# Modulation sums turned by transposes, an earlier first weight split, and narrower chunks in a decoder step on one core

## The chip, the cores and the metric

The kernel runs on one core of one Trainium2 chip. TensorE (PE in the profile) multiplies, VectorE (DVE), ScalarE (ACT) and GpSimd (POOL) do the element-wise work, SyncE (SP) issues most DMAs. The metric is the device time of one execution in microseconds. Three runs of the kernel before took 1521.88, 1522.25 and 1519.98 us; the median is 1521.88.

## The reference

One layer of a decoder runs for 256 prompt tokens and 8 sample tokens that share all weights. The parts that matter here are the modulation and the large products:

```
mod = silu(c) @ w_ada + b_ada                    # 2048 x 12288
sh1, sc1, gt1, sh2, sc2, gt2 = split(mod, 6)     # parts 0 to 5
h = rmsnorm(x, g) * (1 + sc1) + sh1
q, k, v, u, ga, gb = split(h @ w_in)             # 2048 x 9216
...                                              # attention, pooling, gates: mix
x = x + gt1 * (mix @ w_out)                      # 2048 x 2048
h2 = rmsnorm(x, g2) * (1 + sc2) + sh2
x = x + gt2 * (square(relu(h2 @ w_mlp_up)) @ w_mlp_down)   # 2048 x 8192 and back
```

After that comes a final RMSNorm. All is float32, and the caches of keys, values and pooling rows are outputs too.

## The kernel before, in words

Activations lie transposed: 16 blocks of 128 model rows (kt) by N = 264 columns, 256 of the prompt and 8 of the samples. Every weight tile is loaded by `load` (L218) into one of 5 buffers named raw, 1 MB at most. `split_w` (L226) splits 1024 columns of it into hi (a cast on ACT, L230) and lo (a subtraction on DVE, L231), in one of 3 buffers each. `mm3` (L238) then makes one product as three: hi by hi, hi by lo, lo by hi (L241 to L243). Results lie in 5 PSUM buffers (`mm_tile`).

The modulation is a product with 9 columns (one prompt, 8 samples). TensorE holds 32 columns of cT and streams w_ada past it, in four column groups at once, so the result pa has 9 used rows in each of four 32-row groups. `ada_block` (L251) copies pa to SBUF on ACT. A function `finish` turns it into columns: each block of 128 columns is multiplied by a 0/1 selection matrix, sel2 or sel4 (L311, L356). `set_mods` (L256) adds b_ada on DVE, and for the two scale parts (1 and 4) adds 1 and multiplies by the norm weight. `ada_pair` (L271) makes parts 0 and 1 for the rows of one chunk; `ada_part` (L330) makes one whole later part in 16 steps. Two tiles of w_ada are consumed in one burst (L263). A `finish` waits in `pending` until `flush` runs, at the next load of a modulation tile or before a use.

The first 40 of the 72 column blocks of w_in are computed in chunks of kt: CHUNKS = (1, 1, 2, 4, 4, 4), at L487. A chunk of n rows of blocks goes over all 40 column blocks, n kt deep, and adds its part sums to qkv and up in SBUF. In chunk 0 ACT writes every block (L503). In chunks up to PI = 2 every third block goes through ACT and POOL (L506, L507), all others through DVE (L509, L511). While chunk i runs, `ada_pair` for chunk i + 1 is fed between its units (L527 to L533), and before the last unit `mod_in` makes the rows of h for chunk i + 1: on DVE x times R (L460), on ACT scale and shift (L464), on DVE the sample columns (L465, L466), then `split_x` into hi on ACT and lo on DVE (L235, L236). The first `mod_in(0)` stands ahead of the loop at L520, after the first `ada_pair`, six warm-up transposes (L440) and the row statistics.

The last chunk, the gates, and the projections of the pooling and attention branches are woven with the steps of the later modulation parts in the order 2, 4, 3, 5 (`late`, L519). The output projection (L902) has 16 units and takes a late step after every second one, WO = (1, 2). `need(3)` at L904 then makes sure that part 3 is there. Its columns are appended to h2 (L905, L906), and the MLP starts; its first 512 columns use rows that are not yet normalised, and correct the result later. In the MLP one late step follows every third unit, TW = (1, 3); behind the last part come copies of the caches.

The program's instructions are not issued strictly in the order written: a planner orders each engine's queue by the written order and by what it reckons to be ready, and the engines then work each queue in order. `issue_after` pins one behind another.

Of the kernel before, what the change touches and what calls it, by code (L numbers as in the profile page):

```python
# [22 lines left out]
F32 = mybir.dt.float32  # L23
# [17 lines left out]
CHUNKS = (1, 1, 2, 4, 4, 4)  # L41
# [5 lines left out]
WO = (1, 2)  # L47
TW = (1, 3)
MB = 5
PI, PM = 2, 3  # L50
# [5 lines left out]
def _consts():  # L56
# [12 lines left out]
    sel2, sel4 = np.zeros((128, 18)), np.zeros((128, 36))  # L69
    for g in range(4):  # L70
        for j in range(9):
            sel2[32 * g + j, g // 2 * 9 + j] = 1
            sel4[32 * g + j, g * 9 + j] = 1
    put("sel2", sel2)
    put("sel4", sel4)
# [49 lines left out]
def step_kernel(ctx, tc, x_prompt, x_sample, vectors, c_sample, kv0, kv1, kv2, state_pool, w_ada, w_in, w_up_attn,  # L125
# [37 lines left out]
    def con(name, rows=128):  # L163
        a, n = CONSTS[name]
        i = sum(a >= m for m in _MARKS)
        a -= ([0] + _MARKS)[i]
        return ctiles[i][:rows, a:a + n]
# [3 lines left out]
    sel2, sel4 = con("sel2"), con("sel4")  # L171
# [83 lines left out]

    def set_mods(part, d0, m, p):  # L256
        n = m.shape[1]
        nc.vector.tensor_add(m, p, bT[:, part * 16 + d0:part * 16 + d0 + n, None].to_broadcast([128, n, 9]))
        if part in (1, 4):
            gv = (g_mix if part == 1 else g_mlp)[:, d0:d0 + n, None].to_broadcast([128, n, 9])  # L260
            nc.vector.scalar_tensor_tensor(m, m, 1.0, gv, op0=OP.add, op1=OP.mult)
# [9 lines left out]
    def ada_pair(d0, n, per=2):  # L271
# [34 lines left out]
        def finish():  # L306
            sel = sel2 if n == 1 else sel4
            f = sel.shape[1]
            p = mm_tile()[:, :cols // 128 * f].rearrange("p (a b) -> p a b", b=f)
            for j in range(cols // 128):  # L310
                nc.tensor.matmul(p[:, j], sb[:, j * 128:(j + 1) * 128], sel, start=True, stop=True)  # L311
            for g in range(0, 4, 2 if n == 1 else 1):
                part, half = divmod(g, 2)
                dd = d0 + half * (cols // 128)
                c = g // 2 * 9 if n == 1 else g * 9
                m = mods[:, part * 16 + dd:part * 16 + dd + cols // 128]
                set_mods(part, dd, m, p[:, :, c:c + 9])
# [12 lines left out]
    def ada_part(part):  # L330
# [22 lines left out]
        def finish():  # L353
            p = mm_tile()[:, :144].rearrange("p (j g i) -> p g j i", j=4, g=4)
            for j in range(4):
                nc.tensor.matmul(p[:, :, j], sb[:, j * 128:(j + 1) * 128], sel4, start=True, stop=True)  # L356
            ready.add(part)
            for g in range(4):
                set_mods(part, 4 * g, mods[:, part * 16 + 4 * g:part * 16 + 4 * g + 4], p[:, g])
# [6 lines left out]
    nc.vector.tensor_copy(bT, p1)  # L366
    p1 = px([128, 128])
# [119 lines left out]
    def in_chunk(i):  # L487
        d0, n = starts[i], CHUNKS[i]
        w = 2048 // n
        for c0 in range(0, NB1 * 128, w):  # L490
            ww = min(w, NB1 * 128 - c0)
            v = load(w_in[d0 * 128:(d0 + n) * 128, c0:c0 + ww], n, ww)
            for q0 in range(0, ww, 1024 // n):
                wq = split_w(v[:, :, q0:q0 + 1024 // n])
                for j in range(8 // n):
# [6 lines left out]
                    if i == 0:  # L502
                        nc.scalar.activation(dst, ps, AF.Copy, scale=sc)  # L503
                    elif i <= PI and blk % PM == 1:
                        t = spare[:, blk // PM % 3]
                        nc.scalar.activation(t, ps, AF.Copy, scale=sc)  # L506
                        nc.gpsimd.tensor_add(dst, dst, t)  # L507
                    elif blk < 12:
                        nc.vector.scalar_tensor_tensor(dst, ps, sc, dst, op0=OP.mult, op1=OP.add)  # L509
                    else:  # L510
                        nc.vector.tensor_add(dst, dst, ps)  # L511
# [5 lines left out]

    starts = [sum(CHUNKS[:i]) for i in range(len(CHUNKS))]
    late = chain(*[ada_part(p) for p in (2, 4, 3, 5)])  # L519
    mod_in(0)  # L520
    for i, n in enumerate(CHUNKS):
        units = -(-n * NB1 // 16)
        if i + 1 < len(CHUNKS):
# [3 lines left out]
            for u, _ in enumerate(in_chunk(i)):  # L527
# [542 lines left out]
```

## Time and profile before

| | |
|---|---|
| median of three runs | 1521.88 us |
| profiled execution | 1521.63 us |
| its span, first to last instruction | 1519.9 us |
| busy: TensorE, weight loads, DVE, ACT, POOL | 1492.5, 1401.5, 860.4, 665.6, 86.4 us |
| mean granted TensorE clock | 0.994 of full |
| DMA | 377.63 MB, mean 248 GB/s |

Rows of a timeline give the start and the length in us, the engine, the line, what is written and read, a count (x), and in brackets how long the engine stood idle before and what ended that. Rows with A:B give busy time and, as (x), instructions of PE, weight load, DVE, ACT and POOL in a stretch, then the granted clock, the busy share of the DMA engines and GB/s. SPq is SP's DMA queue, with the time an issue took.

### The profile page before, as it was taken

The numbers are of one execution on the slowest core, as the hardware profiler recorded it, in microseconds if no ns is written. First come the engines' busy times: TensorE is split into PE (matmuls) and PEld (weight loads), VectorE is DVE, ScalarE is ACT, GpSimd is POOL, SyncE is SP. The second block draws the span as 40 slices with busy tenths as digits, with TensorE's granted clock in tenths as the row PEclk, the third lists the DMA queues.
The fourth block names the chain that finished last, engine by engine and source line by source line (L and its number), as shares of the span: only waits on it lengthen the run. The fifth ranks groups of instructions, "written<-read, shape, count | busy, mean of one in ns | idle before, by whom it ended". The sixth has DMA issues, their size and how long they took to land.

```text
span 1519.9 us, 29037 instructions
## 1 busy us (share of the span) xinstructions
PE 1492.5 (98%) x12349; PEld 1401.5 (92%) x12349; DVE 860.4 (57%) x1358; ACT 665.6 (44%) x985; POOL 86.4 (6%) x147
## 2 busy tenths in 40 slices
PE   7999999999999999999999999999999999999997
PEld 6889999877799988999899999999999999999997
DVE  4766656544466436765765445545555455555765
ACT  6543433344434534454554444344343443434455
POOL 0320000010011000300000000000010000100000
PEclk9999999999999999999999999999999999999998
DMA  9898788887797778767666666666567585777641
GB/s 287 305 334 295 258 315 282 300 291 269 270 317 255 263 261 305 280 248 251 206 223 229 232 235 228 230 234 229 189 230 239 201 297 175 260 239 241 237 139 58
DMA packets 161395, 377.63 MB, mean 248 GB/s; under 512 B 7234, under 2 KB 25170, under 8 KB 151657
## 3 DMA queue, kind: packets, MB, share of 16 engines
q1 hardware_dynamic: 151616, 340.02, 65.1%
q0 software_dynamic: 4064, 33.05, 6.0%
q10 hardware_dynamic: 5584, 2.69, 0.6%
q8 instruction: 97, 1.59, 0.4%
q14 instruction: 34, 0.27, 0.1%
HBM read 370.75 MB, written 26.15 MB: 261 GB/s over the span
## 4 chain that ended last, share of the span: by engine, by line
PE 95%; ACT 2%; DMA 2%; DVE 0%; issue 0%; ACTq 0%; SPq 0%
PE mm L241 29%; PE mm L242 28%; PE mm L243 28%; PE pa L339 4%; PE pa L289 2%; DMA raw<-in_w_in_dram 1%; DMA raw<-in_w_ada_dram 1%; ACT whi L230 1%; PE px L624 1%; ACT qkv L503 1%; PE px L642 0%; PE px L637 0%; PE px L982 0%; PE px L430 0%; PE px L803 0%; PE mm L356 0%
## 5 line engine op out<-in xcount | busy, mean ns | idle before, releaser
L231 DVE TENSOR_TENSOR wlo<-raw,whi 128x1024 fp32r<-128x1024 f32 x448 | 552.0, 1233 | 479.3 <-ACT whi L230 478.7
L230 ACT CAST whi<-raw 128x1024 fp32r<-128x1024 f32 x448 | 469.2, 1049 | 646.6 <-PE mm L242 554.6
L241 PE MATMUL mm<-hhi,whi 128*128 128x264 f32 x1152 | 331.8, 290 | 3.3 <-ACT whi L230 3.3
L242 PE MATMUL mm<-hlo,whi 128*128 128x264 f32 x1152 | 329.6, 287 | 0.0
L243 PE MATMUL mm<-hhi,wlo 128*128 128x264 f32 x1152 | 324.8, 285 | 0.6 <-DVE wlo L231 0.6
L241 PE MATMUL mm<-h2hi,whi 128*128 128x264 f32 (+1 forms) x1024 | 292.6, 286 | 1.5 <-ACT h2hi L235 1.5
L242 PE MATMUL mm<-h2lo,whi 128*128 128x264 f32 (+1 forms) x1024 | 292.3, 286 | 0.0
L243 PE MATMUL mm<-h2hi,wlo 128*128 128x264 f32 (+1 forms) x1024 | 292.0, 285 | 0.0
L243 PE MATMUL mm<-ffhi,wlo 128*128 128x264 f32 x1024 | 291.9, 285 | 0.0
L242 PE MATMUL mm<-fflo,whi 128*128 128x264 f32 x1024 | 291.6, 285 | 0.0
L241 PE MATMUL mm<-ffhi,whi 128*128 128x264 f32 x1024 | 291.6, 285 | 0.0
L241 PEld LDWEIGHTS mm<-hhi,whi 128*128 128x128 f32 x1152 | 217.5, 189 | 21.5 <-issue 14.4
L242 PEld LDWEIGHTS mm<-hlo,whi 128*128 128x128 f32 x1152 | 218.3, 189 | 1.8 <-DVE gate_a L511 1.3
L243 PEld LDWEIGHTS mm<-hhi,wlo 128*128 128x128 f32 x1152 | 216.5, 189 | 1.4 <-DVE wlo L231 1.1
L241 PEld LDWEIGHTS mm<-h2hi,whi 128*128 128x128 f32 x1024 | 193.7, 189 | 5.8 <-ACT whi L230 4.2
L241 PEld LDWEIGHTS mm<-ffhi,whi 128*128 128x128 f32 x1024 | 193.5, 189 | 2.5 <-ACT whi L230 2.5
L242 PEld LDWEIGHTS mm<-fflo,whi 128*128 128x128 f32 x1024 | 193.5, 189 | 0.0
L243 PEld LDWEIGHTS mm<-h2hi,wlo 128*128 128x128 f32 x1024 | 193.2, 189 | 0.0
L242 PEld LDWEIGHTS mm<-h2lo,whi 128*128 128x128 f32 x1024 | 193.2, 189 | 0.0
L243 PEld LDWEIGHTS mm<-ffhi,wlo 128*128 128x128 f32 x1024 | 192.4, 188 | 0.0
L241 PE MATMUL mm<-mhi,whi 128*128 128x264 f32 x256 | 73.2, 286 | 0.0
L242 PE MATMUL mm<-mlo,whi 128*128 128x264 f32 x256 | 72.7, 284 | 0.0
(269 smaller groups left out, 1337.8 us busy)
## 6 DMA issues: line engine op xcount, KB each, us to landing
raw<-in_w_in_dram SPq DMA_DIRECT2D x71, 1024.0 KB, 7.3
raw<-in_w_ada_dram SPq DMA_DIRECT2D x64, 1024.0 KB, 5.1
raw<-in_w_mlp_up_dram SPq DMA_DIRECT2D x64, 1024.0 KB, 5.6
raw<-in_w_mlp_down_dram SPq DMA_DIRECT2D x64, 1024.0 KB, 5.0
raw<-in_w_ada_dram SPq DMA_DIRECT2D x64, 512.0 KB, 7.8
raw<-in_w_out_dram SPq DMA_DIRECT2D x16, 1024.0 KB, 7.0
cv<-in_cache_kv_w_dram POOLq DMA_DIRECT2D x5, 1024.0 KB, 9.1
raw<-in_w_up_pool_dram SPq DMA_DIRECT2D x4, 1024.0 KB, 7.0
```

The lines of the kernel that those rows point to most:

```text
L230: nc.scalar.copy(hi, v)
L231: splits.append(nc.vector.tensor_sub(lo, v, hi.bitcast(F32)))
L241: nc.tensor.matmul(ps, wh, x[0][:, kt, :n], start=start, stop=False)
L242: nc.tensor.matmul(ps, wh, x[1][:, kt, :n], start=False, stop=False)
L243: nc.tensor.matmul(ps, wl, x[0][:, kt, :n], start=False, stop=stop)
L289: i = nc.tensor.matmul(pa[32 * g:32 * g + 32, :cols], cT[:, kt], src, start=done[g] == 1, stop=done[g] == each, tile_position=(0, 32 * g))
L339: i = nc.tensor.matmul(pa[32 * g:32 * g + 32], cT[:, kt], v[:, 0, g * 512:(g + 1) * 512], start=done[0] == 1, stop=done[0] == KT, tile_pos ...
L503: nc.scalar.activation(dst, ps, AF.Copy, scale=sc)
L624: nc.tensor.matmul(p, qkv[:, hd, qt * 128:(qt + 1) * 128], qkv[:, 12 + hd, :nk * 128], start=True, stop=True)
```

## The change

The selection products of all chunks but the narrow first two become transposes: `turn` writes one 128 x 128 transpose for each block of columns, and `set_mods` reads the 9 used columns at steps of 32. sel4 goes. The 1 of the scale parts is added to b_ada once, on POOL, so that `set_mods` multiplies by the norm weight with a plain product. Chunks become 1, 1, 2, 2, 2, 4, 4, and the path through ACT and POOL serves chunks 1 to 4. In chunk 0 every second block is written by DVE. The first tile of w_in is loaded and its first 1024 columns are split ahead of the first rows of h, and `first_rows` makes these: ACT writes hi of the prompt columns at once, DVE makes the sample columns, then the full value again and lo. The output projection takes two late steps after every three units.

```diff
--- before.py
+++ after.py
@@ -38,16 +38,16 @@
 EPS = 1e-6
 NEG = -1e30
 
-CHUNKS = (1, 1, 2, 4, 4, 4)
+CHUNKS = (1, 1, 2, 2, 2, 4, 4)
 NB1 = 40
 START = 7
 LAG = 3
 REST = 17
 UPR = 1
-WO = (1, 2)
+WO = (2, 3)
 TW = (1, 3)
 MB = 5
-PI, PM = 2, 3
+PI, PM = 4, 3
 WARM = 6
 
 CONSTS = {}
@@ -66,13 +66,11 @@
 
     i = np.arange(128)
     put("ident", np.eye(128))
-    sel2, sel4 = np.zeros((128, 18)), np.zeros((128, 36))
+    sel2 = np.zeros((128, 18))
     for g in range(4):
         for j in range(9):
             sel2[32 * g + j, g // 2 * 9 + j] = 1
-            sel4[32 * g + j, g * 9 + j] = 1
     put("sel2", sel2)
-    put("sel4", sel4)
     put("one", np.ones((128, 1)))
     put("grp", (i[:, None] // 16 == np.arange(8)[None, :]) * 1.0)
     marks = [at]
@@ -168,7 +166,7 @@
 
     ident = con("ident")
     one = con("one")
-    sel2, sel4 = con("sel2"), con("sel4")
+    sel2 = con("sel2")
 
     adap = ctx.enter_context(tc.tile_pool(name="adap", bufs=1))
     gapool = tc.tile_pool(name="gap", bufs=1)
@@ -253,12 +251,19 @@
         nc.scalar.copy(sb[:, :cols], src[:, :cols])
         return sb
 
+    def turn(sb, n):
+
+        p = mm_tile(n * 128).rearrange("p (j c) -> p j c", j=n)
+        for j in range(n):
+            nc.tensor.transpose(p[:, j], sb[:, j * 128:(j + 1) * 128], ident)
+        return p
+
     def set_mods(part, d0, m, p):
         n = m.shape[1]
         nc.vector.tensor_add(m, p, bT[:, part * 16 + d0:part * 16 + d0 + n, None].to_broadcast([128, n, 9]))
         if part in (1, 4):
             gv = (g_mix if part == 1 else g_mlp)[:, d0:d0 + n, None].to_broadcast([128, n, 9])
-            nc.vector.scalar_tensor_tensor(m, m, 1.0, gv, op0=OP.add, op1=OP.mult)
+            nc.vector.tensor_mul(m, m, gv)
 
     def burst(raws, emit):
 
@@ -304,17 +309,18 @@
         sb = ada_block(pa, cols)
 
         def finish():
-            sel = sel2 if n == 1 else sel4
-            f = sel.shape[1]
-            p = mm_tile()[:, :cols // 128 * f].rearrange("p (a b) -> p a b", b=f)
-            for j in range(cols // 128):
-                nc.tensor.matmul(p[:, j], sb[:, j * 128:(j + 1) * 128], sel, start=True, stop=True)
-            for g in range(0, 4, 2 if n == 1 else 1):
+            nb = cols // 128
+            if n == 1:
+                p = mm_tile()[:, :18].rearrange("p (a b) -> p a b", b=18)
+                nc.tensor.matmul(p[:, 0], sb[:, :128], sel2, start=True, stop=True)
+                for part in range(2):
+                    set_mods(part, d0, mods[:, part * 16 + d0:part * 16 + d0 + 1], p[:, :, part * 9:part * 9 + 9])
+                return
+            p = turn(sb, nb)
+            for g in range(4):
                 part, half = divmod(g, 2)
-                dd = d0 + half * (cols // 128)
-                c = g // 2 * 9 if n == 1 else g * 9
-                m = mods[:, part * 16 + dd:part * 16 + dd + cols // 128]
-                set_mods(part, dd, m, p[:, :, c:c + 9])
+                dd = d0 + half * nb
+                set_mods(part, dd, mods[:, part * 16 + dd:part * 16 + dd + nb], p[:, :, 32 * g:32 * g + 9])
 
         pending.append(finish)
         yield
@@ -351,12 +357,10 @@
         sb = ada_block(pa, 512)
 
         def finish():
-            p = mm_tile()[:, :144].rearrange("p (j g i) -> p g j i", j=4, g=4)
-            for j in range(4):
-                nc.tensor.matmul(p[:, :, j], sb[:, j * 128:(j + 1) * 128], sel4, start=True, stop=True)
+            p = turn(sb, 4)
             ready.add(part)
             for g in range(4):
-                set_mods(part, 4 * g, mods[:, part * 16 + 4 * g:part * 16 + 4 * g + 4], p[:, g])
+                set_mods(part, 4 * g, mods[:, part * 16 + 4 * g:part * 16 + 4 * g + 4], p[:, :, 32 * g:32 * g + 9])
 
         pending.append(finish)
         yield
@@ -364,6 +368,8 @@
     p1 = px([128, 96])
     nc.tensor.transpose(p1, vr[:96, 1], ident[:96, :96])
     nc.vector.tensor_copy(bT, p1)
+    for part in (1, 4):
+        nc.gpsimd.tensor_scalar(bT[:, part * 16:part * 16 + 16], bT[:, part * 16:part * 16 + 16], 1.0, None, op0=OP.add)
     p1 = px([128, 128])
     nc.tensor.transpose(p1, vr[:, 0], ident)
     nc.vector.tensor_copy(gvec, p1)
@@ -484,14 +490,21 @@
     spare = ga_flat[:, 8 * N:11 * N].rearrange("p (s n) -> p s n", s=3)
 
 
-    def in_chunk(i):
+    def in_load(i, c0):
+        d0, n = starts[i], CHUNKS[i]
+        ww = min(2048 // n, NB1 * 128 - c0)
+        return load(w_in[d0 * 128:(d0 + n) * 128, c0:c0 + ww], n, ww)
+
+    def in_chunk(i, begun=None):
         d0, n = starts[i], CHUNKS[i]
         w = 2048 // n
         for c0 in range(0, NB1 * 128, w):
             ww = min(w, NB1 * 128 - c0)
-            v = load(w_in[d0 * 128:(d0 + n) * 128, c0:c0 + ww], n, ww)
+            v, w0 = (begun or (None, None)) if c0 == 0 else (None, None)
+            if v is None:
+                v = in_load(i, c0)
             for q0 in range(0, ww, 1024 // n):
-                wq = split_w(v[:, :, q0:q0 + 1024 // n])
+                wq = w0 if q0 == 0 and w0 else split_w(v[:, :, q0:q0 + 1024 // n])
                 for j in range(8 // n):
                     blk = (c0 + q0) // 128 + j
                     ps = mm_tile()
@@ -499,7 +512,9 @@
                         mm3(ps, wq, slice(j * 128, j * 128 + 128), kk, h, d0 + kk, kk == 0, kk == n - 1)
                     dst = qkv[:, blk] if blk < 36 else up[:, blk - 36, 16:]
                     sc = HD ** -0.5 if blk < 12 else 1.0
-                    if i == 0:
+                    if i == 0 and blk % 2:
+                        nc.vector.tensor_scalar(dst, ps, sc, None, op0=OP.mult)
+                    elif i == 0:
                         nc.scalar.activation(dst, ps, AF.Copy, scale=sc)
                     elif i <= PI and blk % PM == 1:
                         t = spare[:, blk // PM % 3]
@@ -515,16 +530,31 @@
         tmp = gate_a[:, 4 * (i % 2):4 * (i % 2) + CHUNKS[i]]
         modulate(tmp, h[0], h[1], starts[i], CHUNKS[i], 0, 1, R)
 
+    def first_rows():
+
+        tmp, full = gate_a[:, 0], gate_a[:, 1]
+        hi, lo = h[0][:, 0], h[1][:, 0]
+        nc.vector.tensor_mul(tmp, xT[:, 0], R)
+        A, B = mods[:, 16], mods[:, 0]
+        nc.scalar.activation(hi[:, :T], tmp[:, :T], AF.Identity, scale=A[:, 0:1], bias=B[:, 0:1])
+        nc.vector.tensor_mul(full[:, T:], tmp[:, T:], A[:, 1:])
+        nc.vector.tensor_add(full[:, T:], full[:, T:], B[:, 1:])
+        nc.vector.tensor_copy(hi[:, T:], full[:, T:])
+        nc.vector.tensor_scalar(full[:, :T], tmp[:, :T], A[:, 0:1], B[:, 0:1], op0=OP.mult, op1=OP.add)
+        nc.vector.tensor_sub(lo, full, hi.bitcast(F32))
+
     starts = [sum(CHUNKS[:i]) for i in range(len(CHUNKS))]
     late = chain(*[ada_part(p) for p in (2, 4, 3, 5)])
-    mod_in(0)
+    v = in_load(0, 0)
+    begun = (v, split_w(v[:, :, :1024]))
+    first_rows()
     for i, n in enumerate(CHUNKS):
         units = -(-n * NB1 // 16)
         if i + 1 < len(CHUNKS):
             n1 = CHUNKS[i + 1]
             nxt = ada_pair(starts[i + 1], n1)
             fed = 0
-            for u, _ in enumerate(in_chunk(i)):
+            for u, _ in enumerate(in_chunk(i, begun if i == 0 else None)):
                 while fed < min(2 * n1, -(-2 * n1 * (u + 1) // (units - 1))):
                     next(nxt)
                     fed += 1
```

## Rows read from the trace of the kernel before

**Rows 1.** The page: busy time, share of the span and instructions of each engine.
```profile
PE 1492.5 (98%) x12349; PEld 1401.5 (92%) x12349; DVE 860.4 (57%) x1358; ACT 665.6 (44%) x985; POOL 86.4 (6%) x147
```

**Rows 2.** Stretches of the span, with the columns told above.
```profile
20.00:40.00 20.00, 17.02 (x165) 15.67 (x156) 8.64 (x15) 15.73 (x41) 0.00 (x0) 0.91 0.83 270
40.00:60.00 20.00, 18.80 (x230) 17.72 (x223) 15.15 (x31) 12.00 (x27) 7.75 (x10) 1.00 0.92 316
60.00:80.00 20.00, 18.02 (x190) 15.56 (x185) 13.70 (x30) 7.88 (x14) 5.84 (x7) 0.91 0.77 268
...
720.00:740.00 20.00, 17.82 (x126) 15.21 (x125) 13.46 (x42) 9.37 (x21) 0.19 (x1) 0.91 0.61 211
...
115.00:720.00 605.00, 604.14 (x4970) 543.26 (x4969) 345.20 (x540) 250.82 (x336) 41.77 (x62) 1.00 0.80 279
740.00:1500.00 760.00, 759.98 (x6220) 746.31 (x6219) 426.36 (x613) 335.20 (x482) 19.51 (x50) 1.00 0.65 219
...
30.00:40.00 10.00, 9.32 (x99) 8.43 (x100) 3.68 (x3) 9.27 (x26) 0.00 (x0) 1.00 0.56 201
60.00:65.00 5.00, 3.02 (x74) 2.75 (x69) 3.44 (x6) 2.55 (x4) 1.74 (x2) 0.99 0.97 311
```

**Rows 3.** The same view around the first fall of the clock.
```profile
24.00:27.00 3.00, 3.00 (x14) 3.00 (x15) 2.40 (x3) 1.10 (x3) 0.00 (x0) 0.50 1.05 320
27.00:28.00 1.00, 1.00 (x9) 1.00 (x8) 0.00 (x0) 1.00 (x5) 0.00 (x0) 0.80 1.17 294
```

**Rows 4.** The timeline at the start of the first chunk; the first row is the issue of the first w_in tile, the last one, from the view of DMA issues between 8 and 12 us, gives its size and the time from issue to landing.
```profile
11.93 2.01 SPq L221 DMA_DIRECT2D raw<-in_w_in_dram  x1
20.64 0.27 ACT L253 COPY adasb<-pa 128x128 f32<-128x128 f32 x1 [1.88 <-PE pa L289]
21.20 0.42 PE L440 MATMUL px<-cst,R 128*128 128x128 f32 x2
21.39 0.24 DVE L258 TENSOR_TENSOR mods<-mm,bT 128x9 f32<-128x9 f32 x2 [0.48 <-PE mm L311]
21.88 0.60 ACT L464 ACTIVATE gate_a<-gate_a,mods 128x256 f32<-128x256 f32 x1 [0.97 <-DVE mods L261]
22.51 0.41 ACT L235 CAST hhi<-gate_a 128x264 fp32r<-128x264 f32 x1
22.82 1.99 ACT L230 CAST whi<-raw 128x1024 fp32r<-128x1024 f32 x2
23.92 0.56 PE L241 MATMUL mm<-hhi,whi 128*128 128x264 f32 x1 [2.29 <-ACT whi L230]
...
raw<-in_w_in_dram SPq DMA_DIRECT2D x1, 1024.0 KB, 8.2
```

**Rows 5.** The timeline of chunk 0 and its end; the last row is the group of column blocks that DVE adds to qkv in the later chunks (busy time, mean ns of one, idle before).
```profile
26.71 4.59 ACT L503 ACTIVATE qkv<-mm 128x264 f32<-128x264 f32 x14 [1.90 <-PE mm L243]
32.29 0.39 PE L241 MATMUL mm<-hhi,whi 128*128 128x264 f32 x1 [0.68 <-ACT whi L230]
33.78 1.23 DVE L231 TENSOR_TENSOR wlo<-raw,whi 128x1024 fp32r<-128x1024 f32 x1 [0.29 <-ACT whi L230]
35.03 6.04 SPq L297 DMA_DIRECT2D raw<-in_w_ada_dram  x4
39.98 2.03 ACT L230 CAST whi<-raw 128x1024 fp32r<-128x1024 f32 x2
42.23 0.40 PE L311 MATMUL mm<-cst,adasb 128*128 128x18 f32 x2 [1.20 <-ACT adasb L253]
...
L511 DVE TENSOR_TENSOR qkv<-qkv,mm 128x264 f32<-128x264 f32 x104 | 43.2, 426 | 29.9 <-PE mm L243 29.7
```

**Rows 6.** The timeline at the boundary of chunks 1 and 2.
```profile
61.58 1.99 ACT L230 CAST whi<-raw 128x1024 fp32r<-128x1024 f32 x2 [1.17 <-DMA raw<-in_w_in_dram]
63.79 0.41 PE L311 MATMUL mm<-cst,adasb 128*128 128x36 f32 x2 [1.98 <-ACT adasb L253]
```

**Rows 7.** The timeline at the boundary of chunks 2 and 3: TensorE's three waits.
```profile
101.78 0.64 PE L311 MATMUL mm<-cst,adasb 128*128 128x36 f32 x4 [0.49 <-ACT adasb L253]
102.72 0.39 PE L241 MATMUL mm<-hhi,whi 128*128 128x264 f32 x1 [0.31 <-ACT whi L230]
104.51 0.39 PE L243 MATMUL mm<-hhi,wlo 128*128 128x264 f32 x1 [0.56 <-DVE wlo L231]
```

**Rows 8.** The timeline from the output projection to the MLP: the projection's last product and TensorE's two long waits.
```profile
726.15 0.28 PE L243 MATMUL mm<-mhi,wlo 128*128 128x264 f32 x1
...
730.71 1.08 PE L356 MATMUL mm<-cst,adasb 128*128 128x36 f32 x8 [0.69 <-ACT adasb L253]
733.92 1.05 PE L241 MATMUL mm<-h2hi,whi 128*128 128x274 f32 x3 [1.48 <-ACT h2hi L235]
```

**Rows 9.** Turning and its bursts: a group of instructions (busy time, mean ns of one, idle before), one case of eight selection products from the chain of work, eight transposes of x from the timeline, and one burst each of a chunk of 2 and of 4.
```profile
L356 PE MATMUL mm<-cst,adasb 128*128 128x36 f32 x32 | 4.0, 271 | 0.7 <-ACT adasb L253 0.7
1408.74 0.81 PE mm L356 x8
16.98 1.15 PE L430 MATMUL px<-cst,qkv 128*128 128x128 f32 x8
59.85 1.95 PE L289 MATMUL pa<-raw,cT 128*32 128x128 f32 x64
83.56 1.93 PE L289 MATMUL pa<-raw,cT 128*32 128x256 f32 x32
```

## The prediction

> **What bounds the kernel now.** I read the page's busy shares first, then the 20-us stretches, then the timeline of each stretch that isn't full. TensorE is busy 98% of the span and no other engine over 57% [rows 1], so time can only be won where TensorE stands still, where its clock is down, or by giving it less to do. The stretches say where it stands still [rows 2]: 2.98 us missing in 20-40, 1.20 in 40-60, 1.98 in 60-80 and 2.18 in 720-740; three waits of 1.36 together lie at 101-105 [rows 7]. The stretches from 115 to 720 and from 740 to 1500 miss 0.9 of 1365 us together [rows 2]; the tail is not touched by the edit. In 20-40, 60-80 and 720-740 the mean granted clock is 0.91 besides. One such fall in detail [rows 3]: three us at 0.50, the lower of the two levels (1.2 GHz), then one at 0.80: 3 x 0.5 + 0.2 = 1.7 us of full-speed work lost, as each of the three falls costs (0.09 x 20 = 1.8 by the coarse rows). So pauses and falls are worth at most 9.7 + 5.1 = 14.8 us.
>
> What TensorE did before a fall: at 21.62 it stopped for 2.3 us [rows 4], and the clock fell on resuming; after 1.98 us it fell [rows 6], and after 0.69 and 1.48 us close together [rows 8]; after 1.20 us it did not [rows 5], nor after 0.49, 0.31 and 0.56 us within 3 us [rows 7]. Here, then, pauses of 1.2 us and less left the clock alone, and those of about 2 us cost it.
>
> **Start of the first chunk.** Before: the modulation sums are copied (ACT 20.64), turned, added on DVE; then ACT works in a row: scale and shift 21.88 (0.60), cast to hi 22.51 (0.41), weight cast 22.82-23.9, and TensorE starts at 23.92 [rows 4]. `first_rows` drops the 0.41 cast by writing hi at once, which leaves about 0.5 with all else in order. The best case puts the weight cast into ACT's gap from 20.91 to 21.88 (0.97 long; the cast takes 1.0): TensorE then waits only for hi, at 22.5, a gain of 1.4. The weights land at 11.93 + 8.2 = 20.1 us [rows 4], so the gap can be used. But `split_w` issues a DVE subtraction of 1.2 us too, and DVE has to add and multiply the modulation sums from 21.39 and then make the sample columns of hi. If the subtraction comes between, hi is ready at 23.2 to 23.7, a gain of 0.2 to 0.7. Bounds 0 and 1.4; I take 0.5, nearest to the row of the removed cast. The pause then still lasts 1.8 us, nearer to the 1.98 that lost the clock than to the 1.20 that kept it, so I leave the fall in.
>
> **Chunk 0.** ACT alone evacuates all 40 blocks: 14 in 4.59 us, and the next weight cast waits behind them until 31.3, which costs TensorE 0.68 us at 32.29 [rows 5]. With every second block on DVE, one 1024-column piece costs ACT 1.0 + 4 x 0.33 = 2.3 us and DVE 1.23 + 4 x 0.43 = 2.95 us [rows 5] against 24 products on TensorE at 0.122 (760 us for 6220 records [rows 2]), 2.9 us, so this pause goes (0.7). At 42.23 TensorE waits 1.20 us for the copy of the next modulation sums, which stands on ACT behind two weight casts of 2.03 us [rows 5]. With ACT ahead of its work, the floor of copy and hand-over stays, 0.49 at the later boundary [rows 7]: gain 0.7. DVE is the new nearest limit here; if it were late by 0.1 us a piece, five pieces would give back 0.5. Together 1.4 (0.5 to 1.9).
>
> **Boundary of chunks 1 and 2.** TensorE waits 1.98 us, and the clock falls: the copy of the sums stands behind two weight casts, and these wait for a weight tile that lands at 61.5 [rows 6]. So DMA ends last here. It was half idle at 30-40 (0.56 of its engines) and full at 60-65 (0.97) [rows 2]: the issue at 35.03 waited for a buffer until the late subtraction at 33.78 ended, at 35.01 [rows 5]. That piece was late because its cast stood behind the evacuations. With these halved the buffer comes free about 3 us earlier against TensorE, and that is about 1 MB less in the queue at 61. The blocked casts then come off in time, the 0.49 floor stays, and the clock holds: 1.98 - 0.5 + 1.7 = 3.2. Bounds: 3.7, and -0.7 if DMA keeps its time while TensorE arrives earlier. I take 3.2; it is the least certain term.
>
> **Chunks of 2 in place of 4.** The boundary of chunks 2 and 3 cost 1.36 us in three waits [rows 7]; fetching half the modulation columns beside it takes 4 MB off DMA. But there are three boundaries out of a chunk of 2 now where there was one. Two at half the 0.49 floor and one (to a chunk of 4, as before, but with DMA no longer behind) at 0.5 make 1.0: gain 0.4. Bounds: 1.4 if all are covered, -2.7 if all three repeat 1.36. TensorE's own work hardly changes: the sums for 4 rows of weights cost two pairs of bursts of 1.95 instead of four of 1.93 [rows 9], so 0.1 more. Forty more evacuations go to DVE, ACT and POOL; a chunk of 2 then costs DVE about 10 x 1.23 + 27 x 0.43 + 4 = 28 us beside 32.8 us on TensorE (240 products at 0.12 and two bursts), so they are covered; without that cover the price would be DVE's excess over 32.8. I book 0.4 together with the shorter accumulation groups; 0 to 0.8.
>
> **Turning the sums.** A selection product shows as two records, 8 in 0.81 us; the later parts have 32 such records [rows 9], and the pairs of one chunk of 2 and three of 4 have 2 + 3 x 4 = 14 by the code: 46 x 0.10 = 4.6 us in a full stream. The transposes number 3 + 4 + 16 = 23 at 1.15 / 8 = 0.14 [rows 9], 3.3 us (at the selection products' pitch 2.3). Gain 1.3 to 2.3; I take 1.5. The two additions to the b_ada tile go to POOL, which is 6% busy [rows 1], in the first microseconds; the sums use that tile from 21.39 [rows 4], so I cost them at nothing; without that cover it would be about the 0.24 of the two small operations at 21.39.
>
> **Output projection and MLP.** The last product of the projection ends at 726.3, and then the sums of part 3 are still to be copied, turned and split before the MLP may start: waits of 0.69 and 1.48, and a fall [rows 8]. `WO` = (1, 2) feeds the 48th step after the last of 16 units; (2, 3) feeds it after the 12th and turns it at the 14th. The wait goes, and so does the fall: 2.18 + 1.7 = 3.9. What comes late next is the row-sum chain, whose products TensorE meets in its queue: about 0.5 by the floor [rows 7]. Two steps of part 5 (one burst, 1.85 us) move from the MLP to here; that is no extra work, and DMA stands at 0.6 in this stretch [rows 2]. So 3.4; bounds 1.5 (the chain's 731 to 733.9 stays as a wait without a fall) and 3.9.
>
> **Sum.** 0.5 + 1.4 + 3.2 + 0.4 - 0.1 - 0.4 + 1.5 + 3.4 = 9.9 us. The profiled execution took 1521.63 us (span 1519.9 and 1.7 around it), the median of the three runs is 1521.88. 1521.6 - 9.9 = 1511.7, and I say 1511.5 us.
>
> **Rivals.** (1) The clock holds at the start too: a pause below 1.2 us, as in the best case. Then 0.9 + 1.7 more: 1509. For it speaks the gap on ACT, against it the subtraction on DVE: one of three orders gives it, and the clock must agree, so 0.17.
> The Trainium skill (TensorE: Matmul & The Clock Gate, Part 4) says that transposes don't count as work for the clock. The last work before the pause is six transposes (the last two in rows 4), and the clock did fall after them, which fits this rule and the bare 2.3 us alike. By the rule this rival would fail even with a short pause, and the time would be the forecast's.
> (2) The boundary of chunks 1 and 2 keeps its wait and its fall, because the planner again puts two casts ahead of the copy and the tile lands no earlier: 1511.5 + 3.2 = 1514.7. The order on ACT in rows 6 speaks for it.
> (3) The MLP start keeps a wait of its row-sum chain with a fall: 3.4 is lost, 1515; with (2) as well, 1518.
> (4) Slower: the narrow chunks make each of the four boundaries out of chunks 1 to 4 repeat rows 6, a copy stuck behind casts that wait for DMA, with a fall: 4 x 3.7 = 14.8 against 3.7 + 1.4 = 5.1 before, so 9.7 lost, while the start, chunk 0, turning and the MLP bring 6.3: about 1525. It decides from the third such boundary on. Against it: at 100-105, with twice the modulation columns to fetch, no clock fell [rows 7].
>
> **Numbers.** Forecast 0.34, rival 1 0.17, rival 2 0.25, rival 3 0.17, rival 4 0.07. The range, 1506 to 1518 us, takes in the best ends of the start, the boundaries and turning, and rivals 1 to 3. A difference of 0.2% (3 us) is what a measurement here tells from none. Rival 4 gives 0.05 slower and 0.02 the same; half of rival 3 (with 2 on top) lies at the edge, 0.07 the same. So faster 0.86, same 0.09, slower 0.05.
>
> **What would show it.** Start: the first product at about 23.4 us, and 1-us rows at 0.50 behind it. Chunk 0: no pause over 0.5. After the sums of chunk 2's rows: a pause under 0.6, the clock at 1.00. Turning: one record per block of columns. 715-740 full, with no row at 0.50. The prediction is wrong if the pauses move to the new boundaries rather than vanish, or if the MLP's first products still wait.

## The result, and the profile after

The changed kernel takes 1508.16 us (median of 4 runs, 1507.92 to 1511.97), the kernel before 1521.08 beside it (4 runs): a ratio of 0.9929, 95% interval 0.9914 to 0.9943. That is 12.9 us faster by the medians, and 10.8 by the ratio (8.7 to 13.1 by its interval). The forecast was 1511.5, 10.1 below the 1521.6 it started from; the range 1506 to 1518 holds the time.

The head of the page of the changed kernel, against [rows 1]:

```profile
span 1506.4 us, 29357 instructions
...
PE 1484.2 (99%) x12454; PEld 1398.6 (93%) x12454; DVE 875.4 (58%) x1404; ACT 668.3 (44%) x992; POOL 114.6 (8%) x175
```

The stretches of the changed kernel (us; busy time and instructions of PE, PEld, DVE, ACT, POOL; granted clock; DMA share; GB/s), against [rows 2]:

```profile
20.00:40.00 20.00, 17.44 (x170) 16.05 (x169) 16.24 (x32) 13.06 (x25) 0.00 (x0) 0.91 0.92 289
40.00:60.00 20.00, 19.18 (x249) 18.03 (x249) 16.61 (x37) 11.10 (x23) 9.49 (x11) 1.00 1.01 333
60.00:80.00 20.00, 19.21 (x198) 18.22 (x198) 16.11 (x34) 9.78 (x16) 6.45 (x8) 1.00 0.87 299
80.00:100.00 20.00, 19.61 (x210) 19.21 (x209) 15.00 (x30) 10.30 (x17) 7.95 (x8) 1.00 0.85 292
100.00:120.00 20.00, 20.00 (x214) 19.66 (x213) 15.10 (x25) 9.02 (x15) 7.93 (x8) 1.00 0.85 291
120.00:140.00 20.00, 19.61 (x229) 18.43 (x227) 15.88 (x31) 10.00 (x18) 10.11 (x8) 1.00 0.84 280
...
160.00:180.00 20.00, 19.51 (x178) 18.37 (x177) 16.37 (x30) 12.31 (x18) 3.90 (x5) 1.00 1.00 356
...
720.00:740.00 20.00, 20.00 (x162) 20.00 (x161) 17.44 (x43) 13.61 (x28) 0.19 (x1) 1.00 0.58 195
```

Two of the three falls of the clock are gone (60-80 and 720-740 stand at 1.00), and 720-740 is full. What is left of standing still is mostly the start: 2.56 of the 5.44 us that these rows miss. The timeline of the changed kernel (start, duration, engine, line, out<-in, count, idle time before and what ended it) shows TensorE's waits, against [rows 4 to 6], and the start of the MLP, against [rows 8]:

```profile
18.48 1.08 PE L294 MATMUL pa<-raw,cT 128*32 128x128 f32 x32
...
20.86 0.60 ACT L539 ACTIVATE hhi<-gate_a,mods 128x256 fp32r<-128x256 f32 x1 [0.97 <-DVE mods L266]
...
21.37 1.98 ACT L228 CAST whi<-raw 128x1024 fp32r<-128x1024 f32 x2
...
22.45 0.59 PE L239 MATMUL mm<-hhi,whi 128*128 128x264 f32 x1 [1.84 <-ACT whi L228]
...
30.40 0.39 PE L239 MATMUL mm<-hhi,whi 128*128 128x264 f32 x1 [0.34 <-ACT whi L228]
...
39.49 0.40 PE L315 MATMUL mm<-cst,adasb 128*128 128x18 f32 x2 [0.38 <-ACT adasb L251]
...
57.79 1.99 ACT L228 CAST whi<-raw 128x1024 fp32r<-128x1024 f32 x2
...
60.00 0.33 PE L258 MATMUL mm<-cst,adasb 128*128 128x128 f32 x1 [0.71 <-ACT adasb L251]
...
61.97 0.39 PE L239 MATMUL mm<-hhi,whi 128*128 128x264 f32 x1 [0.18 <-ACT gate_a L521]
...
64.39 0.75 PE L239 MATMUL mm<-hhi,whi 128*128 128x264 f32 x4 [0.60 <-ACT hhi L233]
...
708.00 0.60 PE L258 MATMUL mm<-cst,adasb 128*128 128x128 f32 x4
...
722.03 0.28 PE L241 MATMUL mm<-mhi,wlo 128*128 128x264 f32 x1
722.15 0.29 PE L239 MATMUL mm<-h2hi,whi 128*128 128x274 f32 x1
```

At 57.79 the two casts no longer wait for a DMA (at 61.58 they did, 1.17 us [rows 6]), but the copy of the sums still stands behind them, and TensorE waits 0.71 instead of 1.98. The sums of part 3 are turned at 708.00, inside the output projection, and the MLP's first product follows the projection's last without a gap.

Where the time came from is best read from landmarks on TensorE (to 0.1 us). The three numbers of before are its first profile and two more of the same code (below); the two of after likewise.

| stage (us) | before | after | gain |
|---|---|---|---|
| start of the program to the first product | 23.9, 23.8, 21.3 | 22.4, 23.4 | see text |
| to the turning of the sums for chunk 1 | 18.3, 18.3, 18.2 | 17.0, 17.1 | 1.3 |
| to the turning of the sums for chunk 2 | 21.6, 21.5, 21.4 | 20.5, 20.5 | 1.0 |
| to the first product of attention | 250.2, 250.2, 250.2 | 247.0, 247.0 | 3.2 |
| to the first product of the output projection | 312.8, 313.6, 312.3 | 311.1, 311.3 | 1.7 |
| to the last product of the MLP | 880.4, 881.6, 880.4 | 875.6, 875.6 | 4.8 |
| first to last product | 1483.3, 1485.3, 1482.5 | 1471.3, 1471.4 | 12.0 |

The first product comes anywhere from 21.3 to 23.9 us in one and the same code, so "first to last product", called the stream below, leaves out one source of spread. It is still no sharp measure: the spans of the three executions of before differ by 5.4 us, their streams by 2.8, nearly all of it behind attention (312.3 to 313.6, and 880.4 to 881.6, where the second profile stood at 0.50 twice as long). The stages from the first product to attention repeat within 0.2 us. So the stages, rather than the whole stream, say what an edit did.

### The profile page after: what moved, and what is told of

Its sections match the earlier page's. It is cut to its first block, busy times and chain, and to the rows that moved or that the text cites. A ratio compares the mean times of both kernels' runs of the same rounds, so it can differ in the third digit from the quotient of the medians.

```text
span 1506.4 us, 29357 instructions
## 1 busy us (share of the span) xinstructions
PE 1484.2 (99%) x12454; PEld 1398.6 (93%) x12454; DVE 875.4 (58%) x1404; ACT 668.3 (44%) x992; POOL 114.6 (8%) x175
## 4 chain that ended last, share of the span: by engine, by line
PE 97%; ACT 1%; DMA 1%; DVE 0%; issue 0%; SPq 0%; ACTq 0%
PE mm L239 29%; PE mm L240 29%; PE mm L241 29%; PE pa L345 4%; PE pa L294 2%; PE px L654 1%; PE px L672 1%; DMA raw<-in_w_ada_dram 1%; PE px L636 0%; ACT whi L228 0%; PE px L1012 0%; PE px L667 0%; PE px L436 0%; PE px L833 0%; PE mm L258 0%
```

## Experiments

Each ratio is to the kernel before as timed beside that kernel: its medians were 1520.44 us for the first four rows, 1520.42 for the change without alternate evacuation and 1520.28 for the others. A stream is that of one profile; "before" in the last column is the first of its three.

| kernel | median us (runs) | ratio to before, 95% | stream, us | against |
|---|---|---|---|---|
| `WO` = (2, 3) alone | 1515.21 (6) | 0.9964 [0.9951, 0.9977] | 1478.3 | before -5.0 |
| alternate evacuation alone | 1517.46 (12) | 0.9982 [0.9971, 0.9992] | 1479.2 | before -4.1 |
| turning alone | 1515.35 (6) | 0.9965 [0.9951, 0.9979] | 1478.4 | before -4.9 |
| narrow chunks alone | 1518.08 (12) | 0.9983 [0.9972, 0.9995] | 1479.1 | before -4.2 |
| first split and first rows alone | 1520.33 (12) | 1.0005 [0.9992, 1.0018] | 1482.9 | before -0.4 |
| change without turning | 1511.61 (5) | 0.9943 [0.9931, 0.9954] | 1474.6 | after +3.3 |
| change without alternate evacuation | 1512.39 (6) | 0.9941 [0.9922, 0.9961] | 1474.5 | after +3.2 |
| change, 22 transposes in the pause | 1508.19 (6) | 0.9923 [0.9911, 0.9934] | 1470.6 | after -0.7 |
| change, 13 products in the pause | 1508.08 (5) | 0.9918 [0.9905, 0.9931] | 1470.3 | after -1.0 |

### Each part alone

**Output projection.**

```diff
-WO = (1, 2)
+WO = (2, 3)
```

> The kernel before with WO = (2, 3) alone. Theory: the wait and the clock fall between the output projection and the MLP go, 3.4 to 4.2 us, so about 1517 where the kernel before takes 1521; TensorE is full from 715 to 745 and no 1-us row stands at 0.50 there. Rival: the row-sum chain takes the place of the wait, and at most 1.5 us are won.

5.2 us by the medians. From the projection's first product to the MLP's last, 880.4 us became 876.6: 3.8, which is the 2.18 of waits and the 1.7 of the fall [rows 2, 8] with nothing in their place. The rest of the 5.0 lies ahead of the edited code: this execution waited 1.33 at the boundary of chunks 1 and 2, without a fall. It also had something that nobody expected. Two views of its stretches:

```profile
20.00:22.00 2.00, 0.27 (x2) 0.27 (x3) 1.26 (x4) 1.97 (x4) 0.00 (x0) 1.00 1.18 293
22.00:24.00 2.00, 2.00 (x15) 1.66 (x15) 2.00 (x2) 1.08 (x3) 0.00 (x0) 1.00 1.10 397
...
98.00:100.00 2.00, 1.44 (x10) 1.23 (x10) 1.32 (x3) 2.00 (x5) 0.00 (x0) 0.88 1.05 387
100.00:102.00 2.00, 2.00 (x11) 2.00 (x11) 1.18 (x3) 1.79 (x2) 0.00 (x0) 0.50 1.05 388
102.00:104.00 2.00, 2.00 (x15) 2.00 (x14) 2.00 (x2) 1.82 (x3) 0.78 (x1) 0.76 0.48 142
```

The pause at the start was 2.30 us, as before (2.29), and the clock held: chunk 0 took 17.1 us up to the turning for chunk 1 instead of 18.3. At 96 to 99 came the same three short waits as in [rows 7], 0.49, 0.31 and 0.56, and there it fell: up to the next turning it took 70.3 us instead of 68.7.

**Alternate evacuation** of the first chunk.

```diff
-                    if i == 0:
+                    if i == 0 and blk % 2:
+                        nc.vector.tensor_scalar(dst, ps, sc, None, op0=OP.mult)
+                    elif i == 0:
```

> The kernel before with every second block of chunk 0 written by DVE, alone. Theory (the copy at the boundary of chunks 1 and 2 is late because DMA is late, and DMA is late because chunk 0's evacuations hold the casts): 1.4 us in chunk 0, and the boundary at 60 to 64 us loses its fall as well, 3 to 4.6 us in all. Rival (the planner's order there decides): 0.7 to 1.4 us, the wait of 1.98 us and the fall stay.

3.0 us by the medians. The pauses of 0.68 and 1.20 shrank to 0.31 and 0.38, and the wait at the boundary of chunks 1 and 2 to 0.80, with no fall. Chunk 0 took 17.1 us instead of 18.3.

**Turning**, with the additions to the b_ada tile: `turn` in place of the `sel4` products.

```diff
-                nc.tensor.matmul(p[:, :, j], sb[:, j * 128:(j + 1) * 128], sel4, start=True, stop=True)
...
+            nc.tensor.transpose(p[:, j], sb[:, j * 128:(j + 1) * 128], ident)
```

> The kernel before with transposes for the selection products (and the 1 added to b_ada once), alone. Theory: 23 transposes for 46 records, 1.3 to 2.3 us faster, the waits at 42, 63, 101 and 730 us as before. Rival: transposes are no work for the clock, and a stretch that keeps its clock in the kernel before falls to 0.50 (100 to 107 us): no gain.

5.1 us, far more than the 1.3 to 2.3 of its own arithmetic. Much of the excess lies at the boundary of chunks 1 and 2: a wait of 0.72 in place of 1.98, and no fall, which is worth 1.3 and 1.2 (the price of the fall is worked out below). The remaining 2.4 of its 4.9 us in the stream is just past the bounds. With the clock held, TensorE also met a wait behind the boundary that the kernel before doesn't show:

```profile
64.43 0.63 PE L296 MATMUL pa<-raw,cT 128*32 128x256 f32 x4 [0.51 <-DMA raw<-in_w_ada_dram]
```

**Narrow chunks.**

```diff
-CHUNKS = (1, 1, 2, 4, 4, 4)
+CHUNKS = (1, 1, 2, 2, 2, 4, 4)
...
-PI, PM = 2, 3
+PI, PM = 4, 3
```

> The kernel before with chunks of 1, 1, 2, 2, 2, 4, 4 (and the path through ACT and POOL up to chunk 4), alone. Theory: 0.4 us faster, between 1 us slower and 1 us faster: the three waits of 1.36 us after chunk 2 shrink to the 0.4 floor, and two more boundaries bring 0.4 each. Rival: the boundaries repeat the wait and the fall of the boundary of chunks 1 and 2, several us slower.

2.4 us by the medians, and again a boundary without a fall (a wait of 1.14), 0.8 and 1.2 of the 4.2 us in the stream. Another 0.7 lies between attention and the output projection, which this edit doesn't touch. The rest is TensorE's own work. Groups by line from 20 to 300 us, first of before, then of this kernel (form and count, busy us, mean ns, idle time before):

```profile
L289 PE MATMUL pa<-raw,cT 128*32 128x256 f32 x384 | 24.6, 383 | 0.0
...
L289 PE MATMUL pa<-raw,cT 128*32 128x128 f32 x216 | 7.5, 274 | 0.0
```

```profile
L289 PE MATMUL pa<-raw,cT 128*32 128x256 f32 x256 | 15.5, 382 | 0.0
L289 PE MATMUL pa<-raw,cT 128*32 128x128 f32 x448 | 14.5, 274 | 0.0
```

Before, 24 of the 216 records belong to the first sums, at the window's edge (0.8 us by their share); without them 31.3 us became 30.0. The prediction had 0.1 more here, not 1.3 less. The timeline of the kernel before shows why: a whole wide burst of 32 records takes 1.93 or 1.94 us, but two of its twelve run in pieces, among other products:

```profile
68.78 0.63 PE L289 MATMUL pa<-raw,cT 128*32 128x256 f32 x4
70.02 0.63 PE L289 MATMUL pa<-raw,cT 128*32 128x256 f32 x6
76.11 1.50 PE L289 MATMUL pa<-raw,cT 128*32 128x256 f32 x22
...
177.15 1.05 PE L289 MATMUL pa<-raw,cT 128*32 128x256 f32 x10
189.66 1.50 PE L289 MATMUL pa<-raw,cT 128*32 128x256 f32 x22
```

These two take 2.76 and 2.55. In the kernel with narrow chunks all eight wide bursts and the four added narrow ones run whole.

**Weights split first, and first rows.** `in_load`, the `begun` argument and `first_rows`, with all else as before.

> The kernel before with the first weights split ahead of the first rows, and first_rows, alone. Theory: from the end of the first sums' burst on TensorE to the first product 2.9 us instead of 3.35, so 0.5 us faster and nothing else. Rival: the weight cast goes into ACT's gap, and the stretch takes 2.0 us, 1.4 us faster.

No difference in time. The mechanism is there, though. The end of the burst and the first product of this kernel:

```profile
18.94 1.08 PE L289 MATMUL pa<-raw,cT 128*32 128x128 f32 x32
...
22.91 0.39 PE L241 MATMUL mm<-hhi,whi 128*128 128x264 f32 x1 [1.85 <-ACT whi L230]
```

From the end of the burst (20.02) to the first product it takes 2.89 us, and before 3.35 (20.57 to 23.92). The 0.46 us are below what the medians can tell from nothing, and in this execution the boundary of chunks 1 and 2 waited 2.66 us, 0.68 longer than in [rows 6].

**Why these sums don't add up.** The four streams give 5.0 + 4.1 + 4.9 + 4.2 = 18.2 against 12.0 together. By stage, as gains against the first profile of before (together: the changed kernel), and for the two kernels of the next section as losses against the changed one:

| stage, us | together | `WO` | evacuation | turning | chunks | without turning | without evacuation |
|---|---|---|---|---|---|---|---|
| to the turning for chunk 1 | 1.3 | 1.2 | 1.2 | 0.0 | 0.1 | -0.7 | 1.2 |
| to the turning for chunk 2 | 1.0 | 0.6 | 0.9 | 1.3 | 0.8 | 0.9 | 1.0 |
| to attention | 3.2 | -0.4 | 1.2 | 1.3 | 2.5 | 0.8 | 0.6 |
| to the output projection | 1.7 | -0.2 | 0.8 | 1.9 | 0.7 | 1.4 | 0.1 |
| to the end of the MLP | 4.8 | 3.8 | 0.0 | 0.4 | 0.1 | 1.0 | 0.3 |

The wait at the boundary of chunks 1 and 2 is shorter in all four, and its fall is missing in all four. What that fall costs can be read where nothing else differs. From the turning for chunk 2 to that for chunk 3 the kernel before takes 37.99 us (63.79 to 101.78 [rows 6, 7]); `WO` and alternate evacuation, with the same code there and no fall, take 36.76 and 36.78:

```profile
59.78 0.41 PE L311 MATMUL mm<-cst,adasb 128*128 128x36 f32 x2 [1.33 <-ACT adasb L253]
96.54 0.63 PE L311 MATMUL mm<-cst,adasb 128*128 128x36 f32 x4 [0.49 <-ACT adasb L253]
```

```profile
60.64 0.41 PE L311 MATMUL mm<-cst,adasb 128*128 128x36 f32 x2 [0.80 <-ACT adasb L253]
97.42 0.64 PE L311 MATMUL mm<-cst,adasb 128*128 128x36 f32 x4 [0.49 <-ACT adasb L253]
```

So it costs 1.2 us, not 1.7. Chance is in the sums too: the 1.2 of `WO` in chunk 0 is the clock that held at the start, its -0.4 the fall that came later, and the 0.8 and 0.7 of evacuation and chunks ahead of the projection lie in a stage that neither touches and that varies by 1.3 in the kernel before. Counted once, chunk 0 gives 1.2, the boundary 1.0 of wait and 1.2 of clock, narrow chunks 1.3 (2.5 - 1.2), `WO` 3.8, and turning 2.4 alone or 3.1 undone (below): 10.9 to 11.6 of the 12.0.

### Parts undone

**The change without turning.**

> The changed kernel with the selection products put back (and the 1 added in set_mods again): turning undone alone. Theory: 1.5 us slower than the changed kernel (1.3 to 2.3), TensorE's stretches otherwise alike, so about 1509.7. Rival, after turning alone brought 5 us: 4 to 6 us slower, with more waits at the boundaries of the chunks.

3.4 us slower by the medians (and 3.4 or 3.5 than the two kernels with a filled pause below, which were timed beside it), 3.3 in the stream. 0.95 of this is a longer wait at the boundary (1.66, with a DMA wait of 0.85 ahead of the casts). Against that, this execution kept its clock at the start, behind a pause of 1.84, and its chunk 0 took 16.3 us instead of 17.0. Without both, turning is worth 3.1. From the projection on it takes 876.6 us, as with `WO` alone, so turning is worth 1.0 there; and all profiles of kernels that turn by transposes need 310.9 to 311.3 us from attention to the projection, those that don't 311.6 to 313.6.

**The change without alternate evacuation.**

> The changed kernel with the evacuations of the first chunk all on ScalarE again. Theory (the alternation removes the stall behind the evacuations in this chunk, worth 1.4 us, and the boundary of chunks 1 and 2 has another cause): pauses of about 0.7 and 1.1 us return near 31 and 40, the copy of the sums stands behind two casts, and the time is 1.4 to 2.5 us above the changed kernel (about 1510). Rival (the prediction's own reading: these evacuations are what makes the weights late at the boundary of chunks 1 and 2): the wait of about 2 us on a DMA and the fall of the clock return near 60 as well, 4.6 us or more, about 1513. A third (the evacuations cost nothing with the other parts in place): 1508.

4.2 us slower by the medians, though the intervals of the two ratios overlap; 3.2 in the stream, of which 1.2 in chunk 0 and 1.6 at the boundary and behind it. The boundary, on ScalarE and TensorE:

```profile
59.50 1.99 ACT L228 CAST whi<-raw 128x1024 fp32r<-128x1024 f32 x2 [1.15 <-DMA raw<-in_w_in_dram]
61.39 0.26 ACT L251 COPY adasb<-pa 128x128 f32<-128x128 f32 x1
...
61.70 0.33 PE L258 MATMUL mm<-cst,adasb 128*128 128x128 f32 x1 [1.96 <-ACT adasb L251]
```

The DMA wait, the 1.96 us and the fall (the rows from 63 to 66 stand at 0.50) are back: the rival's picture, with turning and narrow chunks in place. That supports the prediction's link, evacuations in chunk 0 to the late tile at chunk 2, but doesn't prove it. Over all profiles this wait was 0.72 (turning alone) to 2.66 us (first split alone) with the evacuations on ACT, and 0.70 to 1.66 with half of them on DVE, so something else moves it as well.

### The clock at the start

**22 transposes** (`WARM` = 22) in the pause ahead of the first product, and **13 products** with the identity.

```diff
-WARM = 6
+WARM = 22
```

> The changed kernel with 22 instead of 6 transposes ahead of the first product; they fill the pause of 1.8 us there and nothing else is changed. If transposes count as work for the clock, the first products run at full speed in every execution: up to 1.7 us faster than the changed kernel, less where it kept its clock anyway, and the first product no more than 0.2 us later. If they don't count (the Trainium skill, TensorE: Matmul & The Clock Gate, Part 4): the rows behind the first product stand at 0.50 as often as before, no gain.

> The changed kernel with 13 plain products by the identity in place of the 6 transposes, which fill the same pause. If only plain products count as work for the clock: the clock holds here and falls with the 22 transposes. If both count, both hold; if neither holds, the fall is not decided by this pause. Time: up to 1.7 us faster than the changed kernel.

Both held the clock. The kernel with transposes, timeline and then 1-us stretches:

```profile
20.26 2.16 PE L446 MATMUL px<-cst,R 128*128 128x128 f32 x18
22.52 0.39 PE L239 MATMUL mm<-hhi,whi 128*128 128x264 f32 x1
```

```profile
22.00:23.00 1.00, 0.90 (x8) 0.66 (x7) 0.96 (x3) 1.00 (x2) 0.00 (x0) 1.00 1.18 362
23.00:24.00 1.00, 1.00 (x9) 0.78 (x7) 1.00 (x1) 0.42 (x1) 0.00 (x0) 1.00 0.96 386
24.00:25.00 1.00, 0.82 (x5) 0.66 (x5) 1.00 (x2) 0.34 (x2) 0.00 (x0) 1.00 0.99 401
```

The changed kernel stood at 0.50 in 23:24 and 24:25. Yet the stream is only 0.7 and 1.0 us shorter, and the medians are equal to the changed kernel's. TensorE at full speed soon waits (0.82 busy in 24:25). Its weight loads show for what, in the kernel with transposes: DVE's subtraction, and an evacuation on ACT.

```profile
24.17 0.66 PEld L241 LDWEIGHTS mm<-hhi,wlo 128*128 128x128 f32 x5 [0.39 <-DVE wlo L229]
25.10 0.19 PEld L239 LDWEIGHTS mm<-hhi,whi 128*128 128x128 f32 x1 [0.27 <-ACT qkv L518]
```

So this fall is worth less than 1.7: a large part of what it takes, 0.66 us by these two rows, is time in which TensorE would wait anyway. Neither of the two beats the changed kernel.

### The same kernels once more

> The kernel before, unchanged, profiled once more. Theory (which pauses cost the clock, and how long the boundary of chunks 1 and 2 waits, differs from one execution to the next): the first product within 21.5 to 24, the wait near 62 anywhere from 1.1 to 2 us, and at least one of the falls in 20-40, 60-80 and 720-740 is absent or elsewhere. Rival (these are fixed by the code): 23.9, 1.98 us, and falls in the same three stretches.

> The same once more. Theory: as for the second profile of the kernel before, and the two new profiles differ from each other by more than 0.5 us at the first product. Rival: the three profiles agree within 0.2 us at every pause.

> The changed kernel, unchanged, profiled once more. Theory (the fall at the start varies): the pause ahead of the first product is again about 1.8 us, the first product comes at 21 to 24, 2.9 us behind the end of the bursts, and the clock may hold; at 60 the copy stands behind two casts with a wait of 0.6 to 0.8 and no wait for a DMA. Rival: the fall at 23 to 25 comes every time.

The expectation of ever-changing falls was wrong for the kernel before: both new profiles have the falls at 20-40, 60-80 and 720-740, and waits at the boundary of 1.92 and 1.79. Only the first product moved as expected: it came at 23.84 and 21.29. The second profile of the changed kernel repeats the first: a pause of 1.85, a fall behind it, 2.89 us from burst to product, 0.70 at the boundary without a DMA wait.

## Why the prediction was right, and where it was not

- **Start, 0.5.** Right: 0.46, by the removed cast. The pause of 1.84 and the fall behind it came as forecast, and again in the second profile; the first product at 22.45 and 23.37 (forecast 23.4) differs by when the head ended. Rival 1 did not happen, and the two fillers show that the fall was worth 0.7 to 1.0 in the stream and nothing in the medians, not 1.7.
- **Chunk 0, 1.4.** Right: 1.2 alone, 1.3 in the change. No pause over 0.5 is left (0.34, 0.38), and DVE was not late.
- **Boundary of chunks 1 and 2, 3.2.** Too high: 2.1 alone (0.9 of wait, 1.2 of clock), 1.6 by undoing the evacuations. The mis-sized step is the fall, put in at its whole 1.7 of lost work; it cost 1.2 where it can be read alone. Where the clock holds, TensorE can meet waits behind the boundary instead: 0.18 and 0.60 at 61.97 and 64.39 in the changed kernel, 0.51 at 64.43 with turning alone. The evacuations as the cause are supported by undoing them, in one profile. The step between, that the buffer comes free "about 3 us earlier against TensorE", was not what happened. The sums' weights were issued 6.0 us ahead of the end of chunk 1's bursts before (35.03, 41.03) and 6.3 after (32.86, 39.11); the last weight tiles ahead of the wait 8.75 before chunk 2's bursts ended (53.06, 61.81) and 8.78 after (50.51, 59.29). So the last ones were asked for at the same point, and landed sooner: some 8.5 us after the issue before, at most 7.3 after. Why they land sooner is open. It isn't the evacuations alone either, since turning alone showed no DMA wait there and narrow chunks alone only 0.33. Rival 2 was half right: the planner does put both casts ahead of the copy (57.79), and that is the 0.71 that stays instead of 0.5.
- **Narrow chunks, -0.1.** The sign of the sum was wrong: 1.3. The three boundaries out of a chunk of 2 wait 0.39, 0.39 and 0.49 (at 92.68, 126.51 and 164.47), 1.27 against 1.36, so 0.1 was won there and not 0.4. The shorter groups' 0.4, for which the prediction names no row, is not to be found. The bursts take 1.3 us less instead of 0.1 more. The failed step is that all bursts were priced by the whole ones of [rows 9]: 128 wide products fewer take away 9.1 us (24.6 to 15.5), where four times 1.93 is 7.7, since two of the bursts of before ran in pieces and cost 1.4 more.
- **Turning, 1.5 (1.3 to 2.3).** Too low: 2.4 alone, 3.1 by undoing it, both past the upper bound. The number of blocks, 23, is as forecast; the gain of one is 0.10 to 0.13 us and not 0.07. Of the 2.4 and the 3.1, 1.9 and 1.4 lie between attention and the projection, where the kernel before varies by 1.3, so the size is known to about 1 us only. Why it is more was not separated.
- **Output projection to MLP, 3.4.** Nearly its upper bound of 3.9: 3.8. The 0.5 for the row-sum chain was the mis-sized term: no wait is left in 720-740. Rival 3 did not happen.
- **Sum.** 9.9 forecast; 12.0 in the stream and 0.46 ahead of it, in single profiles (10.8 by the ratio of times, 8.7 to 13.1). Narrow chunks were 1.4 too low, turning 0.9 to 1.6, the projection 0.4; the boundary was 1.1 to 1.6 too high and chunk 0 by 0.1 to 0.2. That the sum came so near is luck in part: errors of both signs cancel.
- **Which pause costs the clock.** "Pauses of 1.2 us and less left the clock alone, and those of about 2 us cost it" was a reading of one execution and is wrong as a rule. At the start, 2.29 or 2.30 us lost the clock in six profiles and kept it in that of the `WO` kernel; 1.84 or 1.85 lost it in four and kept it in that of the kernel without turning; 0.49, 0.31 and 0.56 close together lost it once and kept it elsewhere. What is left of it: at the boundary of chunks 1 and 2 every wait of 1.79 or more (five profiles) came with a fall, and none of 1.66 or less.
- **The rule on transposes.** The Trainium skill (TensorE: Matmul & The Clock Gate, Part 4) says of a kernel's transposes that the full clock doesn't engage for them, as they don't count as busy in the same way. As the prediction reads it, the 18 of them that filled the pause should have left a fall. The clock stood at 1.00 from 20 to 25 us. That is one profile, and the unfilled pause of 1.84 kept its clock in one of five, so the rule is not borne out here, and not refuted either.

## What to carry to other kernels

When several edits each take away the same wait, each looks worth the whole of it alone: look up in every trace whether that wait is still there, and book it once. Where the head varies by 2 us from run to run, compare kernels stage by stage behind the first product, and ask of each stage whether the edit touches it at all. A fall of the clock costs its full price only where TensorE wouldn't wait anyway: 1.7 us of lost work cost 1.6 in one place here, 1.2 in another, and 0.7 to 1.0 in a third. A sum that comes out right doesn't show that its terms are.

## What the runs showed of the hardware

The time to the first product varied from 21.3 to 23.9 us between executions of the same code, while the stages behind it repeated within 0.1 to 1.3 us. The clock fell or held at the same pause (2.29 to 2.30 us) in different executions: it fell in six, the three of before among them, and held in one. A fall to 0.50 that takes 1.7 us of full-speed work lengthened its stage by 0.7 to 1.6. The same weight tiles, asked for at the same point against TensorE, landed 1.85 us late in one kernel (the first split alone) and in time in another (turning alone), whose code up to there differs little.
